# Two MLP projections as one row of steps over one set of buffers, with the VectorE and SyncE queues in a written order

## The chip, the cores and the metric

One core of one Trainium2 chip runs the whole kernel. The metric is the device time of one execution in microseconds; lower is better. The core's engines each work through a queue of their own: TensorE (PE, matmuls), VectorE (DVE), ScalarE (ACT), GpSimd (POOL) and SyncE (SP, which here only issues DMAs). They wait for each other through semaphores.

## The reference

A decoder layer of width 1024 for 1024 positions: three branches (mLSTM, differential attention, attention into a memory) are merged and added to x. The change touches only what follows, a squared-ReLU MLP with 4096 hidden channels:

```python
h2 = rms_norm(x, norm_mlp_g[l])
x = x + jnp.square(jax.nn.relu(h2 @ w_up[l])) @ w_down[l]
```

All of it is float32, and the kernel keeps close to that: it splits each operand into a high part `hi` (rounded to the TensorE's format) and a rest `lo`, and makes every product out of three matmuls, hi·hi, hi·lo and lo·hi (`mm3`).

## The kernel before

**Seven products for eight.** Both projections use Winograd's form of Strassen's scheme. A 2 x 2 block product takes seven block products instead of eight, at the price of sums of blocks before and after. One *step* is one block of contraction for one block of output columns: seven products of three matmuls, 21 matmuls of 128x128 by 128x512, one after the other into seven PSUM banks. A *pass* is the row of steps that accumulate in the same seven banks; the up-projection has 64 steps (mostly in passes of four, `u` = 0 to 15), the down-projection 64 more (groups `g` = 0 to 3 of output columns, contraction blocks `q` = 0 to 15).

**Banks.** There are eight. Product j of pass r uses bank (7r + j + 4) mod 8, so the first product of a pass finds a free bank, and product j + 1 needs the bank of product j of the pass before: VectorE or ScalarE must have read that product by then.

**Weights.** A step needs one weight block. SP loads it (`wraw`, 256 KB), POOL forms four sums in it (L1124 to L1127), ScalarE casts it to its high part and VectorE subtracts for the low part (`wo`, L104 and L105; the first ones L111 and L112). This pair is called a split. `W4` in the prediction is the weight of step 4, counted from 0 in the up-projection; the steps of the down-projection count on from 64.

**Up-projection** (`wino`, L1153 to L1240). Its four input blocks X (`xo`) are split once and kept. `xts` are sums of input blocks, two by VectorE alone, one by POOL, one more by VectorE (L1106 to L1109). After a pass, `combine` (L1172) makes four blocks out of the seven banks: one copy on ScalarE and seven adds on VectorE. `use_up` multiplies them by `rb`, the reciprocal norm (VectorE), applies relu and square (ScalarE, eight instructions), forms `xts` of the result and writes everything to DRAM (`r_d`). Block u = 0 is computed in two halves, with a partial result `pt`; then `rb` is made beside the first steps (`rstd`): `px` collects the sums of squares, VectorE copies it to `st` (L1397), POOL takes the reciprocal root (L127, L128), VectorE makes eight diagonals `dg` (L1402), two matmul groups spread them and ScalarE copies them to `rb`.

**Down-projection** (`down`, L1429 on). `xd` are blocks of `r_d`, loaded in parts of 512 to 1024 KB and split like weights. Sixteen passes of four steps go around the four groups, each one block further along q, and wrap around at q = 16, so that the first blocks are loaded a second time. `A` or `acc` are a group's seven accumulators; a pass is *evicted* into them by adds on VectorE (L1543, L1561). In a group's first pass, three are copies on ScalarE (L1541), four add to blocks of x loaded before. A group is closed by seven adds on VectorE (L1563 to L1572) and four output DMAs on SP; the last pass is closed straight from its banks (L1578 on).

**What sets the order.** Only matmuls are held in program order (`pin`). On the other engines a list scheduler orders the instructions by its own costs when the kernel is built. It put down's first loads and splits into the end of the up-projection, and weight splits between the evictions of a pass. The two projections have separate pools; a weight's split leads its step by three in the up-projection and by two in the down-projection.

Of the kernel before, what the change touches and what calls it, by code (L numbers as in the profile page):

```python
# [31 lines left out]
def f32(ap):  # L32
    return ap.bitcast(F32)
# [38 lines left out]
class Layer:  # L72
# [109 lines left out]
    def consts(self, tmp):  # L182
# [13 lines left out]
        self.dv = cp.tile([P, 48], F32, name="dv")  # L196
# [903 lines left out]
    PROD = ((0, 0), (1, 2), (4, 4), (5, 5), (2, 6), (3, 3), (6, 1))  # L1100

    def wino_t(self, b, V):

        G = self.nc.gpsimd
        t = self.xtp.tile([P, 4, 512], F32, tag="xt", name=self.name("xts"))
        V.tensor_sub(t[:, 0], b[:, 0], b[:, 1])  # L1106
        G.tensor_sub(t[:, 2], b[:, 2], b[:, 0])
        V.tensor_sub(t[:, 1], b[:, 2], t[:, 0])
        V.tensor_sub(t[:, 3], b[:, 3], t[:, 1])  # L1109
        return t  # L1110

    def wino_x(self, kp, load):

        b = load(kp)
        t = self.wino_t(b, self.nc.vector)
        xo = self.xop[kp].tile([P, 7, 2, 512], F32R, tag="xo", name=self.name("xo"))
        self.split(xo[:, 0:3, 0], xo[:, 0:3, 1], b[:, 1:4])
        self.split(xo[:, 3:7, 0], xo[:, 3:7, 1], t)
        return xo

    def wino_s(self, r):

        G = self.nc.gpsimd
        G.tensor_add(r[:, 4], r[:, 0], r[:, 3])  # L1124
        G.tensor_sub(r[:, 5], r[:, 4], r[:, 1])  # L1125
        G.tensor_sub(r[:, 6], r[:, 1], r[:, 0])  # L1126
        G.tensor_sub(r[:, 7], r[:, 2], r[:, 5])  # L1127

    def wino_steps(self, srcs, wrp, wop, lead):


        raws, W = [], []

        def raw():
            n = len(raws)
            if n < len(srcs):
                r = wrp.tile([P, 8, P], F32, tag="wraw", name=self.name("wraw"))
                self.nc.sync.dma_start(r[:, 0:4], srcs[n])
                self.wino_s(r)
                raws.append(r)  # L1140

        def wsp(n, split=self.split2, more=True):
            m = len(W)
            if m < len(srcs) and m <= n + lead:
                wo = wop.tile([P, 7, 2, P], F32R, tag="wo", name=self.name("wo"))
                split(wo[:, :, 0], wo[:, :, 1], raws[m][:, 1:8])
                W.append(wo)
            if more:
                raw()

        return raw, wsp, W

    def wino(self, ws, load, use, first, parts):  # L1153


        V, A = self.V, self.A
        self.pinned = True

        runs = [(0, (0, 1)), (1, (0, 1, 2, 3)), (0, (2, 3))] + [(u, (0, 1, 2, 3)) for u in range(2, len(ws))]
        raw, wsp, W = self.wino_steps([ws[u][:, kp] for u, kps in runs for kp in kps], self.wrp, self.wop, 3)  # L1160
        X = {}
        raw()
        wsp(0, self.split)
        X[0] = self.wino_x(0, load)
        wsp(0, self.split)
        X[1] = self.wino_x(1, load)
        X[2] = self.wino_x(2, load)
        raw()
        wsp(0, self.split)
        tl = lambda n: self.ev.tile([P, 512], F32, tag=n, name=self.name(n))  # L1170

        def combine(ms, psum):  # L1172

# [13 lines left out]


        todo = {}
        n = -1  # L1190
        for r, (u, kps) in enumerate(runs):
            bank = lambda j: f"p{(7 * r + j + 4) % 8}"
            ps = [self.pw.tile([P, 512], F32, tag=bank(j), name=self.name(f"p{j}")) for j in range(7)]
            for kp in kps:
                n += 1
                if n == 2:
                    X[3] = self.wino_x(3, load)
                w, x = W[n], X[kp]
                for j, (l, q) in enumerate(self.PROD):
                    self.mm3(ps[j], (w[:, l, 0], w[:, l, 1]), (x[:, q, 0], x[:, q, 1]), kp == kps[0], kp == kps[-1])  # L1200
                    if (r, kp, j) in ((0, 1, 1), (1, 1, 6), (1, 2, 6), (1, 3, 3)):
                        first(bank(7))
                if kp != kps[-1]:
                    wsp(n)
                    for f in todo.pop(n, []):
                        next(f)
            if r == 0:
                part = parts()
                for t, m in zip(part, ps):
                    A.copy(t, m)  # L1210
                wsp(n)
            elif r == 2:
                for t, m in zip(part, ps):
                    V.tensor_add(t, t, m)
                wsp(n)


                def whole():
                    c = combine(part, False)
                    yield  # L1220
                    yield from use(0, c)

                next(late)
                g = whole()
                todo.update({n + 1: [late], n + 3: [g], n + 5: [g], n + 8: [g]})
            else:
                cs = combine(ps, True)
                wsp(n)
                g = use(u, cs)
                if r == 1:  # L1230
                    late = g
                else:
                    for f in todo.pop(n, []):
                        next(f)
                    next(g)
                    todo.setdefault(n + 1, []).append(g)
        for g in sum(todo.values(), []):
            next(g)
        self.nwino = len(runs)
# [36 lines left out]
    def tail(self):  # L1276
# [11 lines left out]
        with ExitStack() as c0:  # L1288
            E = lambda *x, **k: c0.enter_context(tc.tile_pool(*x, **k))
            one = E(name="tone", bufs=1)  # L1290
            ones = one.tile([P, P], F32, name="ones")
            G.memset(ones, 1.0)
            rb = one.tile([P, D], F32, name="rb2")
            sp = E(name="ssq", bufs=1)
            ssq = sp.tile([P, D], F32, tag="ssq", name="ssq")
            self.gl = E(name="gl", bufs=2)
# [59 lines left out]
            with ExitStack() as c1:  # L1356
                E = lambda *x, **k: c1.enter_context(tc.tile_pool(*x, **k))
                one_ = lambda n: E(name=n, bufs=1)
                xo2, xo3, wr2, wr3, self.ev, wop1, self.xtp, self.xrp, xo0, xo1, wr0, wr1 = (
                    one_(n)  # L1360
                    for n in ("xo2", "xo3", "wr2", "wr3", "ev", "wop1", "xtp", "xrp", "xo0", "xo1", "wr0", "wr1")
                )
                wop2 = [one_(f"wop2{i}") for i in range(3)]
                self.xop = (xo0, xo1, xo2, xo3)
                self.wrp, self.wop = Ring([wr0, wr1, wr2, wr3]), Ring([wop1, *wop2])
                dp, ap = one_("dgp"), one_("prt")

                def load(kp):
                    b = self.xrp.tile([P, 4, 512], F32, tag="xr", name=self.name("xr"))
                    nc.sync.dma_start(  # L1370
                        b.rearrange("p (k h) n -> p k (h n)", k=2),
                        self.h2d[2 * kp : 2 * kp + 2].rearrange("k p n -> p k n"),
                    )
                    return b

                def use_up(u, cs):

                    b = self.xrp.tile([P, 4, 512], F32, tag="xr", name=self.name("rq"))
                    for i in (1, 3, 2, 0):
                        hf = i % 2  # L1380
                        self.V.tensor_mul(cs[i], cs[i], rb[:, hf * 512 : (hf + 1) * 512])
                        self.A.activation(cs[i], cs[i], AF.Relu)
                        self.A.activation(b[:, i], cs[i], AF.Square)
                    self.A.dma_start(self.rd[u, :, 0:3], b[:, 1:4])
                    yield
                    t = self.wino_t(b, self.V)
                    nc.sync.dma_start(self.rd[u, :, 3:7], t)
                    yield

                def rstd():  # L1390

                    bank = yield
                    ps = self.pw.tile([P, 512], F32, tag=bank, name=self.name("px"))
                    for t in range(NT):
                        self.mm(ps[:, t : t + 1], ssq[:, t * P : (t + 1) * P], ones[:, 0:1], start=True, stop=True)
                    st = dp.tile([P, NT], F32, tag="st", name="st2")
                    V.tensor_copy(st, ps[:, 0:NT])  # L1397
                    self.rsqrt_mean(st, st, D, NT)
                    bank = yield
                    dg = dp.tile([P, NT, P], F32, tag="dg", name="dg")  # L1400
                    for t in range(NT):
                        V.tensor_scalar_mul(dg[:, t], self.ident, st[:, t : t + 1])  # L1402
                    for hf in range(2):
                        bank = yield
                        ps = self.pw.tile([P, 512], F32, tag=bank, name=self.name("px"))
                        for i in range(4):
                            self.mm(ps[:, i * P : (i + 1) * P], ones, dg[:, hf * 4 + i], start=True, stop=True)
# [336 lines left out]
```

## Time and profile before

| | |
|---|---|
| median of 3 runs | 2291.28 us (2290.56 to 2292.64) |
| span of the profiled execution | 2287.7 us, 3.6 us under that median |
| first product of the up-projection | 1639.92 us |
| up-projection ends, down-projection starts | about 1953.3 us |
| last product of the down-projection | about 2283.7 us |
| busy over the span | PE 2203.0, DVE 1388.2, ACT 1012.3, POOL 543.9 us |

The profile is one execution seen by the hardware profiler. Its rows give an engine's busy time, the number and mean length of a kind of instruction, and what ended the idle time ahead of it ("<-DVE acc L1543" is a wait for VectorE's writes to `acc` at line 1543). Names are those of the tiles, written tile first, then what is read.

### The profile page before, as it was taken

What the parts mean: (1) busy time and instruction counts of PE and PEld (TensorE: products, weight loads), DVE (VectorE), ACT (ScalarE), POOL (GpSimd) and SP (SyncE); (2) the same over time, 40 slices, a digit from 0 to 9 for tenths busy, and PEclk for the clock granted to TensorE, in tenths of its full rate; (3) what the DMA queues carried; (4) which work ended last, traced back from release to release, by engine and by line L of the source; (5) the groups of instructions that cost most, each with busy time, mean ns of one, the idle gap of its engine ahead of it and who ended that gap; (6) DMA issues with size and microseconds to landing.
All of it is one profiled execution on the core that took longest, in us unless ns stands there. A gap on an engine that the chain in (4) does not pass through costs nothing.

```text
span 2287.7 us, 30578 instructions
## 1 busy us (share of the span) xinstructions
PE 2203.0 (96%) x11222; PEld 1884.3 (82%) x11222; DVE 1388.2 (61%) x2627; ACT 1012.3 (44%) x1994; POOL 543.9 (24%) x696
## 2 busy tenths in 40 slices
PE   7999999999999999999899999999999999899998
PEld 5788789888898999999787888887787888688777
DVE  6636457552147777777652123454598777856678
ACT  6533445543246666666453112223445444543332
POOL 2100000000011111111000002201576665565553
PEclk9999999999999999999999999999999999999999
DMA  6023212201311110011134225435525444844434
GB/s 242 19 79 102 88 44 83 83 24 62 98 58 33 38 37 24 19 38 33 42 113 168 101 90 174 134 115 173 195 99 204 152 153 148 319 164 152 139 128 166
DMA packets 113781, 247.90 MB, mean 108 GB/s; under 512 B 11065, under 2 KB 19550, under 8 KB 111582
## 3 DMA queue, kind: packets, MB, share of 16 engines
q1 hardware_dynamic: 111326, 233.36, 30.4%
q10 hardware_dynamic: 2304, 12.58, 1.3%
q8 instruction: 88, 1.44, 0.3%
q14 instruction: 63, 0.52, 0.1%
HBM read 178.76 MB, written 67.14 MB: 107 GB/s over the span
## 4 chain that ended last, share of the span: by engine, by line
PE 70%; DVE 14%; DMA 7%; ACT 5%; issue 3%; POOL 2%; SPq 0%; ACTq 0%; DVEq 0%; POOLq 0%
PE mm L91 43%; PE p L91 18%; PE sc L91 4%; ACT dpe L987 2%; PE po L91 2%; DVE sc L979 1%; PE tp L94 1%; DMA wraw<-in_wdown 1%; DMA raw<-in_wd 1%; DVE wo L105 1%; DVE w L112 1%; DVE dpe L1000 1%; DVE daT L112 1%; DVE dq L867 1%; DMA raw<-in_wgate 1%
## 5 line engine op out<-in xcount | busy, mean ns | idle before, releaser
L91 PE MATMUL mm<-w,hT 128*128 128x384 f32 (+3 forms) x2496 | 474.0, 331 | 13.7 <-DVE dq L867 9.0
L91 PE MATMUL mm<-hT,w 128*128 128x512 f32 x1920 | 471.0, 400 | 8.2 <-ACT w L111 5.2
L91 PEld LDWEIGHTS mm<-hT,w 128*128 128x128 f32 x1920 | 360.1, 191 | 84.9 <-ACT w L111 5.8
L91 PEld LDWEIGHTS mm<-w,hT 128*128 128x128 f32 x2496 | 387.4, 189 | 33.3 <-DVE dq L867 13.7
L91 PE MATMUL p<-xd,wo 128*128 128x512 f32 x1344 | 314.1, 395 | 16.2 <-DVE acc L1543 8.5
L91 PEld LDWEIGHTS p<-xd,wo 128*128 128x128 f32 x1344 | 253.9, 190 | 76.3 <-DVE acc L1543 12.4
L91 PE MATMUL p<-xo,wo 128*128 128x512 f32 x1344 | 307.5, 390 | 3.2 <-DVE st L1397 1.8
L91 PEld LDWEIGHTS p<-xo,wo 128*128 128x128 f32 x1344 | 251.4, 188 | 57.9 <-ACT pt L1210 2.2
L112 DVE TENSOR_TENSOR w<-raw,w 128x256 fp32r<-128x256 f32 (+3 forms) x304 | 172.9, 589 | 162.4 <-ACT w L111 161.2
L91 PE MATMUL mm<-kt,w 128*128 128x512 f32 x1152 | 261.3, 389 | 0.0
L91 PEld LDWEIGHTS mm<-kt,w 128*128 128x128 f32 x1152 | 216.2, 188 | 45.0 <-DVE w L112 0.2
L111 ACT CAST w<-raw 128x256 fp32r<-128x256 f32 (+3 forms) x304 | 154.3, 532 | 193.5 <-PE mm L91 112.8
L104 ACT CAST wo<-wraw 128x896 fp32r<-128x896 f32 x122 | 114.8, 942 | 187.7 <-PE p L91 121.9
L105 DVE TENSOR_TENSOR wo<-wraw,wo 128x896 fp32r<-128x896 f32 x122 | 146.2, 1213 | 51.3 <-ACT wo L104 51.1
L1124 POOL TENSOR_TENSOR wraw<-wraw 128x128 f32<-128x128 f32 x128 | 100.9, 788 | 207.3 <-DMA wraw<-in_wdown 132.5
L987 ACT ACTIVATE dpe<-sc,dst,drr 128x256 f32<-128x256 f32 (+7 forms) x128 | 106.6, 833 | 94.0 <-DVE dst L983 92.0
L105 DVE TENSOR_TENSOR xd<-xd 128x1536 fp32r<-128x1536 f32 (+2 forms) x36 | 69.2, 1929 | 69.4 <-ACT xd L104 69.3
L979 DVE CUSTOM_DVE_ANT_0 sc<-sc,tmask 128x256 f32<-128x256 f32 (+7 forms) x128 | 96.9, 757 | 16.5 <-PE sc L91 16.5
L1125 POOL TENSOR_TENSOR wraw<-wraw 128x128 f32<-128x128 f32 x128 | 100.9, 788 | 0.0
L127 POOL TENSOR_SCALAR drr<-drr 128x16 f32<-128x16 f32 x16 | 3.6, 222 | 397.4 <-DVE drr L935 397.4
L1126 POOL TENSOR_TENSOR wraw<-wraw 128x128 f32<-128x128 f32 x128 | 90.7, 708 | 0.0
L127 POOL TENSOR_SCALAR hss<-hss 128x4 f32<-128x4 f32 x8 | 3.3, 409 | 356.2 <-ACT mscr L747 237.6
(319 smaller groups left out, 3084.9 us busy)
## 6 DMA issues: line engine op xcount, KB each, us to landing
wraw<-in_wup SPq DMA_DIRECT2D x64, 256.0 KB, 3.1
r_d<-xts SPq DMA_DIRECT2D x16, 1024.0 KB, 4.2
wraw<-in_wdown SPq DMA_DIRECT2D x64, 256.0 KB, 2.8
xd<-r_d SPq DMA_DIRECT2D x19, 768.0 KB, 6.9
xd<-r_d SPq DMA_DIRECT2D x14, 1024.0 KB, 5.9
raw<-in_wgate SPq DMA_DIRECT2D x48, 256.0 KB, 2.8
gates<-gt SPq DMA_DIRECT2D x48, 256.0 KB, 2.0
raw<-in_wd SPq DMA_DIRECT2D x32, 384.0 KB, 3.2
```

Source lines behind the costliest of these rows:

```text
L91: self.pin(self.nc.tensor.matmul(out, l, r, start=start, stop=stop))
L94: self.pin(self.nc.tensor.transpose(out, x, self.ident))
L104: self.A.copy(hi, src)
L105: self.V.tensor_sub(lo, src, f32(hi))
L111: nc.scalar.copy(hi, src)
L112: nc.vector.tensor_sub(lo, src, f32(hi))
L867: V.scalar_tensor_tensor(out=qT[lo, c], in0=pt[lo], scalar=self.gd[lo], in1=f32(qT[lo, c]), op0=ALU.mult, op1=ALU.subtract)
L979: V.tensor_tensor_reduce(out=sc[:, 0:n], in0=sc[:, 0:n], in1=self.tmask[:, D - n : D], scale=1.0, scalar=-3.0e38, op0=ALU.add, op1=ALU.max ...
L987: nc.scalar.activation(pe[c][:, 0:n], sc[:, 0:n], AF.Exp, bias=t8[:, 2 + c : 3 + c], scale=rr[:, i, c : c + 1], accum_out=t8[:, 4 + c : 5 ...
L1124: G.tensor_add(r[:, 4], r[:, 0], r[:, 3])
L1125: G.tensor_sub(r[:, 5], r[:, 4], r[:, 1])
L1126: G.tensor_sub(r[:, 6], r[:, 1], r[:, 0])
```

## The change

`wino` and `down` become one function, `mlp`, with one set of pools:

- The steps of both projections are one row, numbered from 0 to 127, with one list of weight sources. The weights have three `wo` buffers (four before in the up-projection) and four `wraw`. At the end of step n, first W[n + 2] is split and the load of a further weight is issued, then the banks are evicted or combined, then what `todo` holds for this step is done.
- The instructions that go through `V` and `S` (`InOrder`) stay in program order among themselves on VectorE and SP. `V0` and `S0`, used for X and the reciprocal norm, don't.
- The xd blocks from 1 on use the buffers of the up-projection's X, the first four as it frees them. Their loads and splits, and the loads of x into the accumulators, are put at written steps.
- The down-projection's passes come from a table, `PASSES`: 19 in place of 16, the first ones with 2, 2, 3 and 4 steps and the last with 2, 2, 1 and 4. Every xd block is loaded once.
- Groups 1 and 2 are closed by adds on GpSimd and output DMAs issued there; groups 0 and 3 stay on VectorE and SP.
- The constants tile `dv` is narrower (40 columns, not 48), and the program is built with `dynamic_dma_scratch_size=1024`.

```diff
+    PASSES = (
+        (0, (0, 1)), (1, (0, 1)), (2, (0, 1, 2)), (3, (0, 1, 2, 3)),
+        (0, (2, 3, 4, 5)), (1, (2, 3, 4, 5)), (2, (3, 4, 5, 6)), (3, (4, 5, 6, 7)),
...
+        (0, (10, 11, 12, 13)), (1, (10, 11, 12, 13)), (2, (11, 12, 13, 14)),
+        (0, (14, 15)), (1, (14, 15)), (2, (15,)), (3, (12, 13, 14, 15)),
+    )
+    def mlp(self, one, gl, sp, rb, ssq, E):
...
+        V, S = InOrder(tc, nc.vector), InOrder(tc, nc.sync)
+        V0, S0 = nc.vector, nc.sync
...
+        wrp, wop = Ring([wr0, wr1, wr2, wr3]), Ring([wop1, wop2, wop3])
...
+        ups = [(0, (0, 1)), (1, (0, 1, 2, 3)), (0, (2, 3))] + [(u, (0, 1, 2, 3)) for u in range(2, 16)]
+        srcs = [a["wup"][u][:, kp] for u, kps in ups for kp in kps]
+        nup = len(srcs)
+        srcs += [a["wdown"][g][:, q] for g, qs in self.PASSES for q in qs]
...
+        at(nup - 20, lambda: down_load(0))
+        for i in range(4):
+            at(nup - 15 + 2 * i, lambda: down_split(0))
+        for q in range(1, 16):
+            free = nup - 5 + q if q < 5 else (n0[q - 4][-1])
+            at(free, lambda q=q: down_load(q))
+            for i in (2, 2) if q == 1 else (3, 2):
+                at(n0[q][0] - i, lambda q=q: down_split(q))
...
+            for run in (kps[0:1], kps[1:2], kps[2:4]) if r == last else [(q,) for q in kps]:
+                n += len(run)
+                if n == 2:
+                    up_x(3)
+                for j, (l, x) in enumerate(self.PROD):
+                    for i, q in enumerate(run):
+                        w = W[n - len(run) + 1 + i]
+                        self.mm3(ps[j], (w[:, l, 0], w[:, l, 1]), X[ph, q][x], q == kps[0], q == kps[-1])
...
+                for i in range(len(run)):
+                    wsp()
+                    raw()
+                if run[-1] != kps[-1]:
+                    for f in todo.pop(n, []):
+                        f()
...
+                for j in range(7):
+                    if seen[g] == 1 and j in (0, 2, 3):
+                        A.copy(A_[j], ps[j])
+                    else:
+                        add(A_[j], A_[j], ps[j])
+            for f in todo.pop(n, []):
+                f()
...
+                def close(g=g, A_=A_, fin=fin):
+                    a1, a2, a6, a7, a4, a5, a3 = A_
+                    e = G if g in (1, 2) else S
+                    add = G.tensor_add if g in (1, 2) else V.tensor_add
...
+                at(n + 1, close)
```

Three places show how the instructions move.

**VectorE at the start of the up-projection.** Before, from the split of W3 (`wo_15464`) on; `xts_15538` and `xo_15543` are the sums and splits of the input block X3, `wo_15520` is W4, `wo_15569` W5:

```order
L105 TENSOR_TENSOR wo_15464<-wraw_15421,wo_15464 128x7x128
L1397 COPY st_15488<-px_15479 128x8
L105 TENSOR_TENSOR wo_15520<-wraw_15430,wo_15520 128x7x128
L1402 TENSOR_SCALAR dg<-ident,st_15488 128x128 x2
...
L112 TENSOR_TENSOR xo_15543<-xr_15536,xo_15543 128x3x512
L105 TENSOR_TENSOR wo_15569<-wraw_15467,wo_15569 128x7x128
L112 TENSOR_TENSOR xo_15543<-xts_15538,xo_15543 128x4x512
L1402 TENSOR_SCALAR dg<-ident,st_15488 128x128 x4
```

After, from the copy of px on; `wo_15497` is W3, `xts_15525` and `xo_15530` belong to X3, `wo_15556` is W4 and `wo_15594` W5:

```order
L1277 COPY pt_dg<-px_15470 128x8
L67 TENSOR_TENSOR wo_15497<-wraw_15421,wo_15497 128x7x128
L1281 TENSOR_SCALAR pt_dg<-ident,pt_dg 128x128 x8
L1160 TENSOR_TENSOR xts_15525<-xr_15523 128x512
L1162 TENSOR_TENSOR xts_15525<-xr_15523,xts_15525 128x512
L1163 TENSOR_TENSOR xts_15525<-xr_15523,xts_15525 128x512
L1156 TENSOR_TENSOR xo_15530<-xr_15523,xo_15530 128x3x512
L1156 TENSOR_TENSOR xo_15530<-xts_15525,xo_15530 128x4x512
L67 TENSOR_TENSOR wo_15556<-wraw_15458,wo_15556 128x7x128
L67 TENSOR_TENSOR wo_15594<-wraw_15500,wo_15594 128x7x128
```

The copy of px moved ahead of W3, and W4 moved from ahead of the first `dg` to behind all of them and behind X3.

**POOL at the same place.** After, the rsqrt (L127, L128) stands behind the sums of four weights, W2 to W5; before, those of W4 and W5 stood ahead of the last sums of squares (`ssq`). One row of each weight's four is shown:

```order
L1543 TENSOR_TENSOR ssq<-ssq,sq_15257 128x512
L1141 TENSOR_TENSOR wraw_15391<-wraw_15391 128x128
...
L1141 TENSOR_TENSOR wraw_15421<-wraw_15421 128x128
...
L1141 TENSOR_TENSOR wraw_15458<-wraw_15458 128x128
...
L1141 TENSOR_TENSOR wraw_15500<-wraw_15500 128x128
...
L127 TENSOR_SCALAR pt_dg<-pt_dg 128x8
```

Two weights' sums more stand ahead of the rsqrt than before.

**VectorE in the steady down-projection.** Before, at the end of a pass of group 0; `wo_19431` and `wo_19468` are weights, `xd_19372` is the last part of an xd block, `acc_18044` on are the accumulators:

```order
L105 TENSOR_TENSOR wo_19431<-wraw_19364,wo_19431 128x7x128
L105 TENSOR_TENSOR xd_19372<-xd_19372 128x2x512
L1543 TENSOR_TENSOR acc_18044<-acc_18044,p_2959_19333 128x512
L105 TENSOR_TENSOR wo_19468<-wraw_19402,wo_19468 128x7x128
L1543 TENSOR_TENSOR acc_18045<-acc_18045,p_2960_19334 128x512
L1543 TENSOR_TENSOR acc_18046<-acc_18046,p_2961_19335 128x512
```

After, a pass of group 2; `acc_xt` and `acc_xr` are its accumulators:

```order
L67 TENSOR_TENSOR wo_19440<-wraw_19376,wo_19440 128x7x128
L67 TENSOR_TENSOR wo_19470<-wraw_19411,wo_19470 128x7x128
L67 TENSOR_TENSOR acc_xt<-acc_xt,p_2973_19345 128x512
L67 TENSOR_TENSOR acc_xt<-acc_xt,p_2974_19346 128x512
L67 TENSOR_TENSOR acc_xt<-acc_xt,p_2975_19347 128x512
L67 TENSOR_TENSOR acc_xt<-acc_xt,p_2976_19348 128x512
L67 TENSOR_TENSOR acc_xr<-acc_xr,p_2977_19349 128x512
```

The weight that stood behind the first eviction stands ahead of it, and the evictions follow each other.

More of the change, by code (lines that the diff above doesn't have):

```diff
@@ L1207, in wino @@
[L1207 to L1231, printed above, removed]
+                    up_x(3)
@@ L1595, in run @@
+            self.mlp(one, gl, sp, rb, ssq, lambda *x, **k: c9.enter_context(tc.tile_pool(*x, **k)))
+            c9.close()
     def run(self):
```

506 lines of the change are left out of this document (222 added, 284 removed), and 1 row of the table PASSES.

## The prediction

> **What bounds the kernel now.** I read the page first (busy times), then the list of what TensorE waits for from the MLP on (1500 us to the end), then the table of windows, then the timelines of single engines at the places where TensorE stands.
>
> ```profile
> PE 2203.0 (96%) x11222; PEld 1884.3 (82%) x11222; DVE 1388.2 (61%) x2627; ACT 1012.3 (44%) x1994; POOL 543.9 (24%) x696
> PE p L91 <- DVE acc L1543: 8.5, 7, 2.1
> PE p L91 <- DVE acc L1561: 2.9, 3, 1.1
> PE p L91 <- DVE u L1184: 2.9, 3, 2.0
> PE p L91 <- DVE st L1397: 1.8, 1, 1.8
> ```
>
> TensorE is busy 96% of the span. The products stay the same, 64 steps of 21 matmuls in each projection, so the change can only win TensorE's idle time in the MLP, and any slowed clock behind it. Every large wait names VectorE: an eviction or a combine that gives a PSUM bank back late. Where these lie:
>
> ```profile
> 1653.22:1700.00 46.78, 46.78 (x214) 39.04 (x215) 45.35 (x55) 22.70 (x32) 39.87 (x48) 1.00 0.29 100
> 1700.00:1750.00 50.00, 48.54 (x209) 38.26 (x208) 44.81 (x53) 27.56 (x41) 31.49 (x43) 1.00 0.52 185
> 1750.00:1939.00 189.00, 189.00 (x835) 156.56 (x834) 149.29 (x181) 88.14 (x131) 119.70 (x167) 1.00 0.43 152
> 1939.00:1990.00 51.00, 43.58 (x170) 33.84 (x169) 43.01 (x41) 28.71 (x33) 25.46 (x30) 0.92 0.86 308
> 2100.00:2200.00 100.00, 95.48 (x416) 77.12 (x415) 62.44 (x66) 34.62 (x31) 52.45 (x80) 1.00 0.42 144
> 2200.00:2250.00 50.00, 46.54 (x202) 37.12 (x201) 43.26 (x52) 15.88 (x15) 29.34 (x43) 1.00 0.44 148
> ```
>
> The columns after the length are PE, its weight loads, DVE, ACT and POOL, then the granted clock. A matmul takes 189.00/835 = 0.226 us, a step of 21 takes 4.75 us. VectorE is nearly full (45.35 of 46.78 us, then 44.81 of 50) at the start of the up-projection. TensorE idles 51 - 43.58 = 7.4 us between the projections, and 4.5 + 3.5 = 8.0 us from 2100 to 2250.
>
> **Part A, the start of the up-projection (+8).** VectorE, POOL and TensorE there, before:
>
> ```profile
> 1644.52 0.45 POOL L1124 TENSOR_TENSOR wraw<-wraw 128x128 f32<-128x128 f32 x1
> 1644.93 2.50 POOL L1126 TENSOR_TENSOR wraw<-wraw 128x128 f32<-128x128 f32 x1
> 1653.46 1.65 POOL L128 TENSOR_TENSOR st<-st,mhalf 128x8 f32<-128x8 f32 x1
> 1652.92 0.16 DVE L1397 COPY st<-px 128x8 f32<-128x8 f32 x1
> 1654.21 1.09 DVE L105 TENSOR_TENSOR wo<-wraw,wo 128x896 fp32r<-128x896 f32 x1 [1.13 <-ACT wo L104]
> 1660.07 2.01 DVE L112 TENSOR_TENSOR xo<-xr,xo 128x1536 fp32r<-128x1536 f32 x1
> 1663.27 2.54 DVE L112 TENSOR_TENSOR xo<-xts,xo 128x2048 fp32r<-128x2048 f32 x1
> 1665.74 1.51 DVE L1402 TENSOR_SCALAR dg<-ident,st 128x128 f32<-128x128 f32 x4
> 1653.22 12.97 PE L91 MATMUL p<-xo,wo 128*128 128x512 f32 x56 [1.77 <-DVE st L1397]
> ```
>
> The copy of px frees the bank that step 2 starts on. It moves ahead of the split of W3, so the gap of 1.77 us goes: step 2 starts at 1651.45, and step 4, two steps on, at 1660.95. But the split of W4, which was done at 1655.3, now stands behind all eight dg, three sums xts and both splits of X3. Those need the rsqrt on POOL, and POOL now forms two more weights' sums ahead of it. One weight's four sums cost 1.8 to 3.9 us (four at 0.45, one of them stretched to 2.50 beside VectorE): from 1644.5 on the first at its 3.9 and three more at 2.3 end at 1655.3, and rsqrt with the small step ahead of it about 1657.3, instead of 1653.46 + 1.65 = 1655.1. Then VectorE: eight dg at 0.4 to 0.5 = 3.5, three sums at 0.8 = 2.5, X3's splits 2.01 + 2.54 less overlap 4.4, W4 1.2: ready at about 1669 (1667 to 1671 by the ends of these). TensorE wants W4's low half with the third matmul of step 4, at 1661.4. It stands 7.6 us. Before, it was there at 1653.22 + 9.5 + 0.45 = 1663.2. So TensorE is 5.8 us later, and it restarts slow:
>
> ```profile
> 1597.80 0.73 PE L91 MATMUL mm<-mh,w 128*128 128x512 f32 x2 [2.99 <-DVE w L112]
> 1597.80:1602.04 4.24, 4.24 (x13) 3.34 (x14) 2.79 (x2) 0.00 (x0) 1.09 (x1) 0.65 0.79 242
> ```
>
> After a gap of 2.99 us the clock was 0.65 for 4.24 us: 13 matmuls instead of 4.24/0.226 = 19, or some 1.5 to 2 us lost. Together **+8**, bounds +5 and +10.
>
> **Part B, steps 8 to 19 (+4).** Here VectorE is full, and its order is now fixed: after the four multiplications by rb of a block come one or two weight splits, then the three sums xts, which need ScalarE's squares.
>
> ```profile
> L105 DVE TENSOR_TENSOR wo<-wraw,wo 128x896 fp32r<-128x896 f32 x122 | 146.2, 1213 | 51.3 <-ACT wo L104 51.1
> L104 ACT CAST wo<-wraw 128x896 fp32r<-128x896 f32 x122 | 114.8, 942 | 187.7 <-PE p L91 121.9 <-POOL wraw L1127 50.3 <-POOL wraw L1125 3.8
> L1381 DVE TENSOR_TENSOR c<-c,rb 128x512 f32<-128x512 f32 x30 | 24.7, 822 | 0.0
> L1382 ACT ACTIVATE c<-c 128x512 f32<-128x512 f32 x30 | 19.0, 632 | 61.1 <-DVE c L1381 61.1
> L1543 DVE TENSOR_TENSOR acc<-acc,p 128x512 f32<-128x512 f32 x72 | 44.5, 673 | 0.0
> L105 DVE TENSOR_TENSOR xd<-xd 128x1536 fp32r<-128x1536 f32 x16 | 30.6, 1914 | 6.1 <-ACT xd L104 6.1
> L105 DVE TENSOR_TENSOR xd<-xd 128x2048 fp32r<-128x2048 f32 x12 | 27.5, 2291 | 58.0 <-ACT xd L104 57.9
> L1107 POOL TENSOR_TENSOR xts<-rq 128x512 f32<-128x512 f32 x16 | 28.1, 1754 | 48.9 <-ACT rq L1383 47.9 <-ACT wo L104 1.0
> L1347 POOL TENSOR_TENSOR ssq<-ssq,sq 128x512 f32<-128x512 f32 x14 | 21.1, 1518 | 110.3 <-ACT sq L1346 110.3
> ```
>
> ScalarE's eight relus and squares take 8 x 0.63 = 5.0 us from the first product on, and up to two weight casts (0.94 each) lie among them; VectorE's four multiplications and two splits fill 3.1 + 2.4. It stands about 2 us each at the sums of blocks 1, 2 and 0: 6.5 us. At best nothing waits (then the 50 - 48.54 = 1.5 us that TensorE idles there now go too: -1.5); at the other end all 6.5 and a slow restart of 2 reach TensorE (6.5 + 2 - 1.5 = +7). Behind a standing sum are queued the next weight split and the next combine, and TensorE waits for both. VectorE's rows are those of a 90 to 97% full engine, so I take most of it: **+4**.
>
> **Part C, between the projections (-4).** Before:
>
> ```profile
> 1958.54 0.96 PE L91 MATMUL p<-xd,wo 128*128 128x512 f32 x3 [1.68 <-DVE c L1182]
> 1961.55 14.75 PE L91 MATMUL p<-xd,wo 128*128 128x512 f32 x51 [2.05 <-DVE u L1184]
> xd<-r_d SPq DMA_DIRECT2D x19, 768.0 KB, 6.9
> xd<-r_d SPq DMA_DIRECT2D x14, 1024.0 KB, 5.9
> ```
>
> A split of xd stands in the middle of the last combine; the cost is 7.4 us idle, and 14.75 - 51 x 0.226 = 3.2 us of slow clock, 10.6 in all. In the new order the seven combine adds run through (7 x 0.68 = 4.8 us), then both splits of xd 1 (1.91 + 2.29), four multiplications, W66, W67. With T the end of step 63, the combine is done at T+5, the first split of xd 1 at T+6.9 and the second at T+9.2; step 65 wants them at T+5 and about T+8.3: about 3 us. Then W66 is 0.5 late, and the evictions of pass 0 stand behind W66 and W67 on VectorE, their three copies behind the eight relus on ScalarE: 2 to 3 us more. About 6.5 in all against 10.6: **-4**. Bounds: nothing waits (-10.6), or the weight of step 65, whose load is queued on SP behind the 768 and 1024 KB of xd 1, comes 5 us later (+2).
>
> **Part D, the steady down-projection (-7.5).** In the gaps from 2100 on a weight split stands between evictions:
>
> ```profile
> 2139.63 0.67 DVE L1543 TENSOR_TENSOR acc<-acc,p 128x512 f32<-128x512 f32 x1
> 2141.56 1.19 DVE L105 TENSOR_TENSOR wo<-wraw,wo 128x896 fp32r<-128x896 f32 x1 [1.26 <-ACT wo L104]
> 2142.68 3.66 DVE L1543 TENSOR_TENSOR acc<-acc,p 128x512 f32<-128x512 f32 x6
> 2143.41 0.96 PE L91 MATMUL p<-xd,wo 128*128 128x512 f32 x3 [2.07 <-DVE acc L1543]
> ```
>
> After the first eviction VectorE waited 1.26 us for a weight's cast and split it, and six evictions came late. In the new order that weight stands ahead of the first eviction, and the seven run in one piece, 0.61 us each against 0.68 for the three matmuls of a product. Per pass of four steps, 19 us, VectorE has four weights (4.9), seven evictions (4.7) and one xd (4.2): 13.8. The three additional passes are 21 evictions more, 14 us of VectorE, beside TensorE's products while that slack holds; in the short first passes it doesn't, and what they cost there is in C. The 8.0 us of the two windows go; I leave 0.5 for the passes with an xd load: **-7.5**, bounds -8 and -5.
>
> **Part E, the end (+3).** Closing sums of groups 1 and 2, 14 adds, move from VectorE to POOL, with eight output DMAs.
>
> ```profile
> 2283.92 0.69 DVE L1591 TENSOR_TENSOR acc<-acc,p 128x512 f32<-128x512 f32 x1
> ```
>
> Now VectorE's last add ends at 2284.6, 3.1 us before the span does. POOL can start when the pass of group 1 is evicted, five steps (23.8 us) and the add's own us before that point. The POOL operations of that size above (xts, ssq) took 1.52 and 1.75 us: 14 cost 21 to 25, the sums of the last two weights 4 to 8 more. So POOL is done 25 to 33 us on, 0 to 8 us after VectorE. The transfer behind it is as long as now. **+3**, bounds 0 and +8. The price of a DMA issued on POOL is in no row. (The Trainium skill, "DMA: Bandwidth & Descriptors", section "Anatomy of one DMA — SWDGE (gpsimd) path", gives about 2.0 us plus the bytes over 436e3 per us, by my estimate 2.6 us for 256 KB; no run here shows it yet, and the sum would not change by it.)
>
> The smaller dv, the renamed pools and 16 xd loads in place of 19 are on no path that TensorE waits for, and cost nothing.
>
> Sum: 8 + 4 - 4 - 7.5 + 3 = +3.5. The profiled execution's span is 2287.7 us, 3.6 us under the median of 2291.28 us; I take that offset as the same after: 2287.7 + 3.5 + 3.6 = **2295**.
>
> **The rivals.**
> - *The order works* (faster). TensorE's wait at step 4 lets VectorE catch up, so that B gives only its -1.5; the evictions run in one piece (C -8, D -8), and POOL's tail is covered: with A at +5 it is 2291.3 - 12.5 = 2279. For it: outside the stretches named, TensorE's idle time is already nil. Against: the split of W4 is behind some 12 us of work in the order itself.
> - *POOL's closes set the end* (slower). The 14 adds share the last 24 us with three splits and 17 adds on VectorE; the sum at 1644.93 took 2.50 us beside a split of X on VectorE, where the one ahead of it took 0.45. Stretched by 2 us at four of them, POOL ends 8 us late, E is +8 instead of +3, and with B at its full +7 the time is 2303. It decides from the point where an add costs more than 1.5 us. (The Trainium skill, "GPSIMD Engine Reference", section "8. Key points", speaks against this move too: GpSimd shares its SBUF interfaces with VectorE, above all against instructions with two SBUF inputs, and elementwise work is about twice as fast on VectorE. The 2.50 us agrees.)
> - *A late weight at the head of the evictions* (slower). In front of each pass's evictions VectorE now waits for a weight, in order. If its load, queued on SP behind 1.8 MB of xd, lands 2 us later than the 6.9 us of those, about eight passes lose 2 us each: D is +8 instead of -7.5, 2310.
>
> **How the numbers follow.** The forecast's case, 2287 to 2302, gets 0.43; the order works 0.28; POOL's end 0.19; late weights 0.10. A measurement of this kernel tells about 0.2%, 4.6 us, from no change. Faster: 0.28 and a sliver of the first, 0.30. Same (2286.7 to 2295.9): 0.28. Slower: 0.42. The range leaves out the last tenth on each side: 2275 to 2307; the likeliest case's own is 2287 to 2302.
>
> **What would show it.** A: a TensorE gap of 6 to 9 us on a wo split near 1661, behind the splits of X3. B: gaps of 2 to 5 us within the next 60 us. C: idle time between the projections of 4 to 8 us, clock under 1. D: no gap over 1 us from the fifth pass of the down-projection on. E: POOL's last add after VectorE's. If W4 is there at 1661, A is wrong, and with it the sign of the forecast.

## The result, and the profile after

| kernel | median | range | ratio to before, 95% interval |
|---|---|---|---|
| before | 2290.92 us | 2288.67 to 2292.64 (4 runs) | |
| changed | 2312.93 us | 2303.43 to 2321.24 (4 runs) | 1.0101 [1.0078, 1.0123] |
| changed, measured again later | 2311.15 us | 2307.69 to 2316.90 (5 runs) | 1.0086 [1.0074, 1.0099] beside 2291.28 |

The change costs about 20 us, 0.9 to 1.0%. The forecast was 2295 us with 2275 to 2307: slower, but by 4 us, not by 20.

The first profile is of the slowest run (2321.24 us). Its up-projection already starts 6.8 us later than before (1646.72 against 1639.92 us); in the fourteen profiles taken later, of the changed kernel again and of altered ones, it starts between 1636.5 and 1643.5 us, so those 6.8 us aren't the change. The stages are therefore compared by their own lengths.

What TensorE waits for in the MLP of the changed kernel (us in total, times, longest):

```profile
PE p L91 <- DVE wo L67: 16.7, 5, 7.1
PE p L91 <- DVE acc L67: 6.6, 2, 6.0
PE p L91 <- DVE c L67: 5.9, 2, 3.0
PE p L91 <- DVE xd L67: 1.4, 1, 1.4
PE p L91 <- DVE acc_y L67: 0.8, 1, 0.8
```

Before, the largest was `acc`, evictions, with 8.5 us, and `wo`, a weight's low half, had 0.8 us. Now weights lead. In TensorE's own timeline (start, length, the gap ahead in brackets) the places are:

```profile
1676.23 6.37 PE L91 MATMUL p<-xo,wo 128*128 128x512 f32 x19 [7.08 <-DVE wo L67]
1741.10 4.14 PE L91 MATMUL p<-xo,wo 128*128 128x512 f32 x10 [2.87 <-DVE c L67]
1944.09 28.40 PE L91 MATMUL p<-xo,wo 128*128 128x512 f32 x124 [1.81 <-DVE wo L67]
1994.26 11.32 PE L91 MATMUL p<-xd,wo 128*128 128x512 f32 x42 [5.99 <-DVE acc L67]
2008.59 36.40 PE L91 MATMUL p<-xd,wo 128*128 128x512 f32 x147 [3.02 <-DVE c L67]
2216.81 80.33 PE L91 MATMUL p<-xd,wo 128*128 128x512 f32 x336 [3.62 <-DVE wo L67]
2298.79 0.98 PE L91 MATMUL p<-xd,wo 128*128 128x512 f32 x3 [1.65 <-DVE wo L67]
2302.34 11.40 PE L91 MATMUL p<-xd,wo 128*128 128x512 f32 x37 [2.58 <-DVE wo L67]
```

The first gap is the one that part A forecast. The rest stand at the end of the up-projection, between the projections, and at the end. Several have a slow clock behind them: 19 matmuls in 6.37 us are 2.1 us more than at 0.226 us each, 37 in 11.40 are 3.0 more.

The views that the prediction had not read are SyncE's and ScalarE's. What SyncE's queue stands for, before and then after:

```profile
SPq L1138 <- DVE wo L105: 399.0, 106, 11.3
SPq L1387 <- DVE xts L1109: 63.2, 16, 7.9
```

```profile
SPq L67 <- DVE xts L67: 227.0, 16, 18.7
SPq L67 <- DVE wo L67: 163.7, 39, 15.6
```

Before, SyncE mostly stood with a weight load at its head and no free buffer for it (`wo`): weights were as early as buffers allow. After, it stands 227 us at the sixteen stores of a block's sums (`r_d<-xts`), which wait for VectorE, and the weight loads stand behind them. Between the projections (SyncE's timeline, the changed kernel's first profile):

```profile
1977.03 2.51 SPq L67 DMA_DIRECT2D wraw<-in_wdown  x2
1998.33 0.33 SPq L67 DMA_DIRECT2D r_d<-xts  x1
1998.75 0.38 SPq L67 DMA_DIRECT2D wraw<-in_wdown  x1
1999.22 0.87 SPq L67 DMA_DIRECT2D c<-x_d  x1
2000.15 1.07 SPq L67 DMA_DIRECT2D acc<-x_d  x1
2001.27 1.01 SPq L67 DMA_DIRECT2D acc_rb<-x_d  x2
```

Nothing was issued from 1979.5 to 1998.3 us. The store of block 15 stood at the head, and a weight and the x loads of group 1 came behind it. What VectorE then waited for:

```profile
1991.36 1.39 DVE L67 TENSOR_TENSOR wo<-wraw,wo 128x896 fp32r<-128x896 f32 x1 [4.34 <-ACT wo L1155]
2007.25 0.69 DVE L67 TENSOR_TENSOR acc<-acc,acc_rb 128x512 f32<-128x512 f32 x1 [5.64 <-DMA acc_rb<-x_d]
```

The first holds pass 0's evictions back (TensorE's 5.99 us). Its weight was there: POOL's sums of it ended at 1987.3 us, but ScalarE cast it only at 1990.4 us, behind eight relus and squares. This gap is thus one of VectorE's order, not of SyncE's. The second is an x load that was queued at 2001 (TensorE's 3.02 us).

### The profile page after: what moved, and what is told of

Its sections match the earlier page's. It is cut to its first block, busy times and chain, and to the rows that moved or that the text cites. A ratio compares the mean times of both kernels' runs of the same rounds, so it can differ in the third digit from the quotient of the medians.

```text
span 2319.4 us, 30550 instructions
## 1 busy us (share of the span) xinstructions
PE 2213.6 (95%) x11222; PEld 1890.7 (82%) x11222; DVE 1398.1 (60%) x2625; ACT 996.0 (43%) x1985; POOL 546.3 (24%) x718
## 4 chain that ended last, share of the span: by engine, by line
PE 65%; DVE 14%; DMA 9%; ACT 5%; POOL 3%; issue 2%; SPq 0%; DVEq 0%; ACTq 0%; POOLq 0%
PE mm L91 40%; PE p L91 17%; PE sc L91 4%; ACT dpe L987 2%; DMA raw<-in_wd 2%; DVE wo L67 2%; PE po L91 1%; DMA wraw<-in_wdown 1%; DVE sc L979 1%; PE tp L94 1%; DVE w L112 1%; DVE daT L112 1%; POOL wraw L1142 1%; POOL wraw L1144 1%; DVE dpe L1000 1%
## 5 line engine op out<-in xcount | busy, mean ns | idle before, releaser
L91 PE MATMUL p<-xd,wo 128*128 128x512 f32 x1344 | 320.7, 401 | 20.7 <-DVE wo L67 7.8
L91 PEld LDWEIGHTS p<-xd,wo 128*128 128x128 f32 x1344 | 258.8, 194 | 82.5 <-DVE wo L67 9.7
L1155 ACT CAST wo<-wraw 128x896 fp32r<-128x896 f32 x128 | 120.0, 944 | 332.7 <-POOL wraw L1144 199.6
L67 DVE TENSOR_TENSOR wo<-wraw,wo 128x896 fp32r<-128x896 f32 x126 | 159.0, 1273 | 126.9 <-ACT wo L1155 126.9
L1141 POOL TENSOR_TENSOR wraw<-wraw 128x128 f32<-128x128 f32 x128 | 82.5, 645 | 254.3 <-DMA wraw<-in_wup 114.5
L1144 POOL TENSOR_TENSOR wraw<-wraw 128x128 f32<-128x128 f32 x128 | 95.9, 749 | 9.9
L127 POOL TENSOR_SCALAR drr<-drr 128x16 f32<-128x16 f32 x16 | 3.5, 219 | 397.7 <-DVE drr L935 397.7
L1142 POOL TENSOR_TENSOR wraw<-wraw 128x128 f32<-128x128 f32 x128 | 92.7, 725 | 0.0
L127 POOL TENSOR_SCALAR hss<-hss 128x4 f32<-128x4 f32 x8 | 3.3, 410 | 360.3 <-ACT mscr L747 238.0
L91 PEld LDWEIGHTS po<-dv,daT 128*128 128x128 f32 x576 | 74.7, 191 | 12.4 <-DVE daT L112 11.6
```

The lines of the kernel that those rows point to most:

```text
L67: return self.tc.keep_in_program_order(f(*a, **k))
L91: self.pin(self.nc.tensor.matmul(out, l, r, start=start, stop=stop))
L1155: A.copy(hi, src)
```

## The experiments

All stages are read from each run's own profile. "Up" runs from the first product of the up-projection to the first of the down-projection, "down" from there to TensorE's end, "tail" from there to the end of the span. The idle time of TensorE is split into the up-projection, the first 80 us of the down-projection, and the rest.

| run | median us | span of the profile | up | down | tail | idle in up / first 80 / rest | SyncE at xts stores |
|---|---|---|---|---|---|---|---|
| before | 2290.9 | 2287.7 | 313.4 | 330.4 | 4.1 | 3.2 / 7.4 / 8.8 | 63 us |
| changed_again | 2311.15 | 2309.4 | 327.1 | 334.4 | 6.8 | 12.7 / 11.9 / 7.2 | 229 |
| closes_on_vector | 2311.41 | 2307.8 | 328.0 | 335.6 | 5.4 | 13.5 / 11.8 / 8.4 | 231 |
| start_order | 2312.90 | 2299.8 | 322.7 | 332.6 | 6.8 | 9.5 / 10.0 / 7.6 | 226 |
| store_later | 2307.36 | 2307.4 | 327.3 | 330.7 | 5.9 | 11.9 / 6.0 / 7.9 | 85 |
| vector_free | 2311.17 | 2310.3 | 326.9 | 335.2 | 6.5 | 11.8 / 9.6 / 10.3 | 192 |
| sync_free | 2294.70 | 2293.7 | 322.4 | 321.8 | 7.0 | 8.0 / 8.2 / 4.1 | 48 |
| weight_loads_free | 2297.93 | 2295.3 | 323.0 | 325.9 | 7.0 | 8.1 / 9.8 / 4.2 | 42 |
| weights_one_step_earlier | 2294.37 | 2290.0 | 320.9 | 321.0 | 7.5 | 7.5 / 6.4 / 2.7 | 86 |
| evictions_first | 2289.72 | 2282.1 | 319.6 | 320.1 | 5.9 | 7.1 / 3.4 / 5.5 | 43 |
| earlier_and_evictions_first | 2297.97 | 2297.6 | 321.4 | 329.6 | 7.3 | 8.5 / 8.0 / 6.0 | 86 |
| no_written_order | 2283.11 | 2281.3 | 312.9 | 323.3 | 6.5 | 2.5 / 8.8 / 2.4 | 49 |
| no_order_closes_on_vector | 2282.64 | 2278.2 | 312.3 | 321.5 | 5.1 | 1.9 / 8.3 / 0.8 | 49 |
| sixteen_passes | 2292.37 | 2294.1 | 315.4 | 332.9 | 4.1 | 3.0 / 5.5 / 10.2 | 49 |
| no_order_one_step_earlier | 2277.52 | 2271.6 | 313.0 | 315.0 | 5.1 | 2.4 / 4.3 / 0.8 | 52 |

The kernel before had medians of 2290.4 to 2291.9 us beside them. All of these kernels spread over 5 to 18 us from run to run, so differences of medians under 4 us tell nothing. Each row's stages are those of one profiled run. A run's time is 1.8 us more than its span, and the profile of start_order is of its fastest run, 11 us under its median; that of evictions_first is 6 us under.

**The changed kernel again.**

> The changed kernel itself, for a second profile and more times: 2303 to 2321, with the gap ahead of step 4 at 7 us and the waits between the projections in the same places.

As expected: 2307.69 to 2316.90 us, 7.10 us ahead of step 4, the other waits in the same places. Its profile (span 2309.4 us, close to the median) is the one that the table compares with. Against before, the up-projection is 13.7 us longer, the down-projection 4.0 and the tail 2.8. Of these 20.5 us, 12.4 are more idle time of TensorE, 5.4 are matmuls at a slow clock (more busy time for the same matmuls), and 2.8 are the tail.

**Groups 1 and 2 closed on VectorE and SyncE.**

```diff
-                    e = G if g in (1, 2) else S
-                    add = G.tensor_add if g in (1, 2) else V.tensor_add
+                    e = S
+                    add = V.tensor_add
```

> Groups 1 and 2 are closed on VectorE and SyncE again, the rest as in the changed kernel. If POOL's row of closing adds starves VectorE (in the changed kernel two weight splits took 11.3 us together at 2291, 2.4 elsewhere), the last two gaps of TensorE (1.65 and 2.57 us), the slow clock behind them (about 3 us) and the longer end go: 7 to 9 us less than the changed kernel, and the two splits take 1.1 to 1.3 us each. If instead the last two weights came late by their loads, the gaps stay and 14 adds more on VectorE (about 10 us) make the time the same within 3 us or longer.

The time stayed: 1.0101 [1.0080, 1.0122]. VectorE's splits were short again, but the last weight's split now stands behind seven closing adds in the written order, and TensorE waited 4.73 us for it. So POOL's slowing of VectorE is real (below), but putting the adds back brings nothing while the weights' order stays.

**VectorE's order at the start: X3, W4, then dg.**

```diff
-                V0.tensor_scalar_mul(dg[:, t], self.ident, st[:, t : t + 1])
+                V.tensor_scalar_mul(dg[:, t], self.ident, st[:, t : t + 1])
...
-                    up_x(3)
+                    up_x(3, V)
```

> The diagonals dg and the sums and splits of X3 are put into VectorE's written order: X3, then W4, then the eight dg. If the wait at step 4 is what part A says (W4 behind the reciprocal norm), the gap of 7.08 us ahead of step 4 and about 2 us of slow clock go: 7 to 9 us less than the changed kernel. If VectorE's lack of time only shows elsewhere, the gap comes back between step 6 and step 20 and the time falls by less than 3 us.

A miss of both: the gap fell from 7.1 to 4.13 us and stayed at step 4, and the median didn't move (1.0093 [1.0071, 1.0115]; the profiled run is 11 us under it). X3 stands ahead of W4 now, and its splits wait for ScalarE's casts:

```profile
1655.90 1.76 DVE L67 TENSOR_TENSOR xo<-xr,xo 128x1536 fp32r<-128x1536 f32 x1 [1.82 <-ACT xo L1155]
1660.78 2.38 DVE L67 TENSOR_TENSOR xo<-xts,xo 128x2048 fp32r<-128x2048 f32 x1 [3.12 <-ACT xo L1155]
1663.09 1.34 DVE L67 TENSOR_TENSOR wo<-wraw,wo 128x896 fp32r<-128x896 f32 x1
```

**The stores of a block's sums one step later on SyncE.**

```diff
-                S.dma_start(self.rd[u, :, 3:7], sums(b))
+                t = sums(b)
+                at(n + lag + 1, lambda: S.dma_start(self.rd[u, :, 3:7], t))
```

> Only SyncE's order changes: the store of a block's sums (r_d<-xts) stands one step later in the queue, behind one more weight load. If the head of SyncE's queue is what makes weights and x loads late (SyncE stood from 1979 to 1998 for one such store, and from 1935 to 1951 for the one before), the gaps at 1942 (1.8 us) and 2005 (3.0 us) go with their slow clock, 5 to 8 us less. If the lateness is of the transfers themselves, nothing changes beyond 2 us.

The gaps at the end of the up-projection and at the late x load are gone, as the first theory says; of the idle time between the projections 6.0 of 11.9 us are left. The median is 4 to 5 us lower, but the intervals overlap (1.0075 [1.0057, 1.0093] against 1.0086 [1.0074, 1.0099]), so a gain is not shown. The time that SyncE stands at these stores fell from 229 to 85 us, and yet the large loss stayed: the gap ahead of step 4 is still 7.11 us, the last two still 1.68 and 2.58. These stores are the cause of two gaps, not of the whole.

**No written order at all.**

```diff
-        V, S = InOrder(tc, nc.vector), InOrder(tc, nc.sync)
+        V, S = nc.vector, nc.sync
```

> VectorE and SyncE are ordered by the scheduler again; the passes, buffers and POOL closes stay. If the written order is what costs, the time falls to that of the kernel before or under it (2285 to 2293), with the gap ahead of step 4 under 2 us, and weight splits stand between evictions again. If the buffers and the passes cost it, it stays at 2305 to 2320.

0.9972 [0.9961, 0.9984]: 28 us under the changed kernel and 7 under the one before. Buffers, passes and POOL's closes are all still there. So the written order of the two queues is the whole loss, and the rest of the change, taken together, gains.

**Which of the two queues?** VectorE alone set free, then SyncE alone (the line above with one of the two changed).

> SyncE keeps its written order, VectorE is ordered by the scheduler. If VectorE's written order carries the loss (weights ahead of evictions and behind sums that wait for ScalarE and POOL), the time is within 4 us of the kernel with neither order (2283). If SyncE's queue carries half of it, 2293 to 2300.

> VectorE keeps its written order, SyncE is ordered by the scheduler. If VectorE's order carries the loss, the time stays above 2303 and the gap ahead of step 4 of about 7 us stays. If SyncE's queue carries half, 2293 to 2300, with the gaps at the end of the up-projection and of the late x loads gone.

VectorE free: 1.0078 [1.0065, 1.0090], no gain. The gap ahead of step 4 fell to 1.49 us, but TensorE now stands 3.1, 2.1 and 3.3 us between 1863 and 1933 us; the first of these is behind a split of xd whose loads SyncE issued only at 1859 us, after a store. SyncE free: 1.0008 [0.9996, 1.0020], 16 us less, with VectorE's order as it was. The gap ahead of step 4 fell to 1.83 us, because the loads of W4 and W5, and with them POOL's sums, came before the last sums of squares again (issued at about 1490 and 1626 us, not at 1643 and 1645), and the rsqrt earlier; another 1.04 us stand ahead of step 2. The gap of 5.86 us between the projections stays. VectorE's order costs the other 12 us (2294.7 to 2283.1), and only once SyncE is free.

**Closes without written order.**

> No written order, and groups 1 and 2 closed on VectorE and SyncE. If POOL's closes are part of the 7 us that the kernel without written order gains on the one before, this loses them (2287 to 2291). If they cost at the end, it is 2 to 6 us faster than 2283. If VectorE has room for 14 adds more and POOL's end is hidden, the same within 2 us.

0.9960 [0.9949, 0.9972] against 0.9972 [0.9961, 0.9984]: the same. The closes on POOL neither gain nor cost there.

**Weight loads alone taken out of SyncE's order.**

```diff
-        def raw(S=S):
+        def raw(S=S0):
```

> Only the weight loads leave SyncE's written order; stores, xd and x loads and all of VectorE keep theirs. If the loss on SyncE is weight loads queued behind a store that waits for VectorE, the time falls to that of SyncE without any order (2288 to 2298) and SyncE's time in front of stores costs nothing any more. If it is the x and xd loads, it stays above 2303.

1.0025 [1.0012, 1.0038], 13 us less, at the upper end of the first expectation. The x and xd loads and the stores keep their order.

**Every weight load one step earlier, both orders kept.**

```diff
         up_x(1)
         up_x(2)
         raw(S0)
+        raw(S0)
```

> Both orders as in the changed kernel, but one weight load more ahead of the first step, so that every load is queued one step (4.75 us) earlier. If weights are late by a queue that stands some 16 us per store, 4.75 us of lead take back only a part: 2300 to 2309. If the lateness is small and marginal, most of it: 2290 to 2300.

1.0012 [0.9999, 1.0025]: 17 us less for one line. So most of the lateness was less than a step. (The load that is put ahead is that of W4, which so leaves the written order: the gap at step 4 falls to 2.69 us.) ScalarE's row for the casts of weights shows the same from the other side (idle time ahead and what ended it; the changed kernel's second profile, then the kernel without written order):

```profile
L1155 ACT CAST wo<-wraw 128x896 fp32r<-128x896 f32 x126 | 118.0, 944 | 322.2 <-POOL wraw L1144 185.7 <-PE p L91 103.7 <-issue 14.2
```

```profile
L1155 ACT CAST wo<-wraw 128x896 fp32r<-128x896 f32 x125 | 117.8, 943 | 217.9 <-PE p L91 151.1 <-POOL wraw L1141 19.0 <-POOL wraw L1144 11.5
```

In the changed kernel ScalarE waited 186 us for weights that had only just been loaded and summed; without the order it mostly waits for TensorE to free a buffer, which costs nothing.

**Evictions ahead of the weight split (SyncE free).** At the end of a pass of the down-projection the calls of `wsp()` and `raw()` move behind the seven evictions.

> SyncE without written order; VectorE in a written order in which, at the end of a pass of the down-projection, the evictions stand ahead of the weight split. If a weight at the head of the evictions is what VectorE's order costs there (4.2 us of standing for W67 in the run with SyncE free), the gaps of 5.9 and 1.8 us go and the time falls by 6 to 9 us from 2294.7, to 2286 to 2289. If evictions and weights only change places in the loss, the same within 3 us.

0.9993 [0.9980, 1.0005], by the medians 5 us less than with SyncE free alone, a little short of what was expected; the intervals of the two still touch. The gap of 5.86 us between the projections is gone (0.94 us are left), which shows its cause. The one at step 110, near 2181 us (2.0 us), stays, and one of 2.3 us behind `wo` comes up at the end.

**Sixteen passes of four, no written order.**

> No written order, and the down-projection's passes as 16 of four steps over the same blocks instead of the 19 with short first ones. If the short first passes pay, the idle time between the projections grows from 8.6 us by 3 to 10 us and the time is 2286 to 2295. If they only add evictions, 2278 to 2283.

1.0004 [0.9991, 1.0016], 7 to 9 us more than with the 19 passes. The number was right, the place was not: between the projections it idles less (5.5 us), and the loss stands late, from 2120 us on, mostly in waits for `xd` and `wo` (5.5 and 3.3 us over the down-projection). These 16 passes aren't those of the kernel before: all four groups go over the same four blocks, without its shift by one block from group to group. So it isn't shown whether the number of passes or the missing shift costs.

**Both repairs with both orders.**

> Both written orders stay, with the two repairs together: one weight load more ahead of the first step, and evictions ahead of the weight split at the end of a pass. If SyncE's late weights and VectorE's head-of-row weight are separate losses, their gains add: 2294.4 less 4 to 6 us, 2288 to 2291, what is left being the start and the sums that wait for ScalarE. If the earlier load already mends the row (weights are then there when the evictions are), the same as with the load alone, 2293 to 2296.

1.0025 [1.0013, 1.0038]: the gains don't add, so the first expectation fails. The median is 2 us above the second one and 3.6 us above the earlier load alone, whose interval overlaps (1.0012 [0.9999, 1.0025]), so a loss isn't shown either. Evictions first bring nothing where SyncE is in order with earlier loads.

**The best version: no written order, closes on VectorE, loads one step earlier.**

> No written order, closes on VectorE and SyncE, one weight load more ahead: the likely best version. If weights are never late without a written order, 2281 to 2284 as without the load. If they are late between the projections too (8.3 us idle there), 2276 to 2280.

0.9941 [0.9926, 0.9957], 2277.52 us: 14 us under the kernel before. Weights were late between the projections without a written order too (8.3 us idle there, now 4.3): ScalarE's cast of one waited 1.85 us there for POOL's sums, and now such a cast ends 5 us earlier. This kernel differs from the one without written order in the closes as well, which were worth nothing (above).

## Why the prediction was wrong, point by point

The start of each matmul can be compared with that of the same matmul before, counted from the first product of its projection. That splits the whole difference, from the first product of the up-projection to the end of the span, into the prediction's parts (us; the changed kernel's second profile):

| part | forecast | changed kernel | SyncE free |
|---|---|---|---|
| A, to the start of step 8 | +8 | +8.1 | +4.0 |
| B, steps 8 to 19 | +4 | +1.9 | +4.7 |
| the rest of the up-projection | 0 | +3.7 | +0.4 |
| C, steps 64 to 73 | -4 | +1.8 | -2.2 |
| D, steps 74 to 120 | -7.5 | -4.2 | -7.6 |
| E, from step 121 to the end | +3 | +9.2 | +4.2 |
| sum | +3.5 | +20.5 | +3.4 |

In the first profile of the changed kernel C is +5.2 and D -1.5, the others are within 1.4 us of these.

- **The step at fault** is that the prediction's sum reckoned SyncE's queue as if a weight were always there when its split was due, that is, the written order of SyncE's issues at nothing. With that order taken away the sum comes out almost as forecast, +3.4 us (and 2294.70 us by the median, beside 2295), C, D and E each within 2 us. A alone is 4 us smaller, and that the sum agrees to 0.1 us is chance. With the order, the rest of the up-projection, C, D and E together are 19 us worse than forecast. Freeing the queue, freeing the weight loads alone, or one more load ahead take 13 to 17 of the 20 us.
- **What stood in the way** differs by place. At the start it is no store: the loads of W4 and W5 are issued behind those of W2 and W3. At the end of the up-projection and at the x loads it is the stores of a block's sums (without them at the head, in store_later, these two gaps are gone). At the end it is the four output stores of group 0, ahead of the last two weight loads.
- **Part A was right**, in place and size: forecast a gap of 7.6 us at step 4 and 2 of slow clock, measured 7.1 and 2.1. Its cause was half told. The rsqrt came late because POOL had two more weights' sums ahead of it, as forecast, and those stood there because of where SyncE's order put their loads: with SyncE free, they are out of the way again and the gap is 1.8 us with the very same rows on VectorE. (The estimate of the slow restart was rounded up: 13 matmuls in 4.24 us lose 1.3 us at 0.226 us each, not 1.5 to 2.)
- **Part B** (+4): one gap of 2.87 us instead of several, with 1.9 of slow clock; against what TensorE idled there before, +1.9. The rival *the order works* had that right: TensorE's wait at step 4 gave VectorE time. With that wait gone, in the kernel with SyncE free, B is +4.7.
- **Part C failed** (-4 forecast). The first 80 us of the down-projection idle 11.9 us instead of 7.4. The step forecast W66 "0.5 late" and the evictions 2 to 3 us behind W67; W67 alone held them 4.3 us, since its cast stands behind eight relus and squares on ScalarE. That part is VectorE's order, stays with SyncE free (5.86 us) and goes when the evictions stand first. The x loads of group 1, late by SyncE's order, were not in the sum at all.
- **Part D was right in its mechanism and too large in size**: of the 8.0 us of gaps behind evictions, single ones of at most 0.8 us are left, but at step 110 TensorE waits for a weight (2.2 us, 3.6 in the first profile) with a slow clock behind it. The prediction had said no gap over 1 us there. Every profile with VectorE in its written order has this gap (1.6 us and more): the weight's split stands behind seven adds on group 3's accumulators, `acc_y`. With SyncE free they take VectorE from 2190.2 to 2196.3 us, while ScalarE's cast of the weight is done at 2191.6 us.
- **Part E was mis-sized** (+3, measured +9.2): idle 4.2 us instead of 0.8, slow clock 2 to 3, tail 2.8. POOL ended in time, its last add at 2309.0 us and VectorE's at 2316.2 us (first profile); what it cost was VectorE's two last splits, and these stood so late because SyncE's order put the four stores of group 0, which wait for VectorE, ahead of their loads, and POOL's a closing add ahead of their sums. With SyncE free and the closes still on POOL, the last two gaps are 0.84 and 0.53 us. The tail stays long there (7.0 us); with the closes on VectorE it is 5.1 to 5.4. SyncE at the end, in the first profile:

```profile
2276.59 4.44 SPq L67 DMA_DIRECT2D out<-acc  x4
2281.14 0.87 SPq L67 DMA_DIRECT2D wraw<-in_wdown  x2
```

- **The rival that came near was near by luck.** A late weight at the head of the evictions gave 2310 us, with a chance of 0.10, but it put the loss into the steady passes (D at +8) and named the xd loads. D gained, and the loss stands at the start, between the projections and at the end.
- **The gain was there.** Buffers and passes together are worth 7 us without the written order, and 14 with one load more; their shares weren't measured apart.

## What to carry to other kernels

A queue that issues DMAs in order is an engine like any other: before writing its order, ask of each store how long it will stand for its data, and whether the loads behind it can spare that time. The row of what the issuing queue waits for tells where to look, though not what it is worth: in store_later it fell by 144 us and the time by some 4. A prefetch that stands for a free buffer is early enough; one that stands behind a store may not be, and one step more of lead can be cheaper than any reordering. Fix an order by hand only where the scheduler's own is shown to lose.

## What the runs showed of the hardware

VectorE's splits can starve beside POOL. In the changed kernel's end, with POOL adding 128x512 blocks back to back, a split of a weight on VectorE (two inputs in SBUF) took 7.77 us, where the mean of all is 1.27; with the closes on VectorE, and POOL idle, the last two took 1.08 us each:

```profile
2286.78 2.48 DVE L67 TENSOR_TENSOR acc_xt<-acc_xt,p 128x512 f32<-128x512 f32 x4
2290.97 7.77 DVE L67 TENSOR_TENSOR wo<-wraw,wo 128x896 fp32r<-128x896 f32 x1
```

```profile
2292.17 1.29 POOL L1424 TENSOR_TENSOR acc_rb<-acc_rb,c 128x512 f32<-128x512 f32 x1
2293.43 1.28 POOL L1430 TENSOR_TENSOR u<-u,acc_rb 128x512 f32<-128x512 f32 x1
2294.66 0.57 POOL L1418 DMA_DIRECT2D out<-acc_rb  x1
2295.25 1.30 POOL L1427 TENSOR_TENSOR c<-c,acc_rb 128x512 f32<-128x512 f32 x1
```

The evictions just ahead, with one of two inputs in PSUM, kept their 0.6 us each, and POOL's adds their 1.28. The prediction had let POOL stretch. That occurs too: in the same run a sum of 128x128 on POOL took 2.51 us instead of 0.46 beside VectorE's split of an xd block (2266.05 us). (The Trainium skill, "GPSIMD Engine Reference", section "8. Key points", tells of this contention, with instructions on VectorE that have two inputs in SBUF; the rows agree.) A DMA issued on POOL took 0.55 to 0.74 us of POOL's time, and 256 KB landed 2.3 to 2.6 us after its issue (2.1 to 2.2 for SyncE's stores of the output).
